# Three pieces of VectorE work in a two-layer attention kernel, moved to GpSimd and ScalarE

## The chip, the cores and the metric

The kernel runs on one core of one Trainium2 chip. A core has five engines with their own instruction queues, each in order: TensorE (PE in the profile; the loads of its weights, which run beside its matmuls, are listed as PEld), VectorE (DVE), ScalarE (ACT), GpSimd (POOL) and SyncE (SP), which here issues all transfers between HBM and the on-chip memory. The metric is device time of the whole program in microseconds. Before the change the median of three runs is 3306.71 us (3304.67 to 3315.07).

## What is computed

A step of a two-layer backbone on two streams: 256 prompt tokens and 2048 sample tokens, width 1024. The part of the reference that matters here:

```python
def _rmsnorm(x, g):
    xf = x.astype(jnp.float32)
    y = xf * lax.rsqrt(jnp.mean(xf * xf, axis=-1, keepdims=True) + EPS)
    return (y * g.astype(jnp.float32)).astype(x.dtype)
...
def _layer(x, mod, norm_g, w_in, ...):
    shift, scl, gate = jnp.split(mod, 3, axis=-1)
    xn = _rmsnorm(x, norm_g) * (1 + scl) + shift
    proj = xn @ w_in
    q, k, v, z_a, h_c, b_c, c_c, z_c, u_p, z_p = jnp.split(proj, SPLIT_IDX, axis=-1)
    ...
    attn = _attend(q, k_all, v_all) * jax.nn.silu(z_a)
    ...
    out = jnp.concatenate([attn, conv, pool], axis=-1) @ w_out
    return x + gate * out, k, v

def reference(x_prompt, x_sample, cache_k, cache_v, ...):
    ...
    for l in range(DEPTH):
        ...
        z, _, _ = _layer(z, mod, ...)
    y_sample = _rmsnorm(z, final_g)
```

There are 8 query heads of 64 columns that share 2 key and value heads. A sample token attends to 2304 keys (2048 of its own, 256 cached), a prompt token to the 256 of the prompt. Both streams end in a norm with final_g, here called the final norm.

## The kernel before

The program has four phases: for each layer a first one (norm, input projection, the conv and pool branches) and a second one (attention, output projection, and in the last layer the final norm). The first phase of the last layer begins while the tail of the first layer's attention runs.

The second phase works on 4 blocks of 512 query rows, each with 8 heads. One head of one block is a unit of 9 steps, a step being 256 keys; four units of one step carry the prompt's heads. That makes 292 steps per layer. One step has on TensorE four matmuls of scores (st, L1150 and L1151), four of the maxima that a coming unit needs (mx, L1111), and those with the values of the step three before (pv, L1196). ScalarE takes the exponential twice (L1160 and L1162), to P in float32 and ph in float16; ph has buffers for three steps. GpSimd subtracts, pl = P - ph, the low part of P (through the helper padd, L180, so that all its work carries that line), and adds up the pieces of the denominator Z that VectorE reduces (L1182). VectorE also takes the maxima (mr, L1112, from PSUM). At the end of a unit the products with pl follow (L1203).

After a pair of heads its output o is finished in four parts, one step apart, by fin_c: c1 multiplies by the reciprocal denominators on VectorE (L1254), c2 by the gate silu(z) on GpSimd (o<-o,zs), c3 casts the high part mixh on ScalarE (L1261), and c4 subtracts it from o on VectorE, which gives the low part mixl (L1266). There are 20 such pairs in a layer, 40 in the program. The output projection of a block (outproj) takes high and low parts as operands. It stands in a list from which one entry is taken per step: its matmuls read weights that SP loads on the way (wo); after each fourth entry VectorE adds the product to the residual (ox, L1327), and at the end of a quarter of the columns SP stores it.

In the last layer the final norm comes after a block's projection. ScalarE has squared the rows (L1330). The list called slow then gives one entry per step: first mean (L1349 to L1351: the sum over the squares, times 1/D, and the making of the list of the root's parts), then the 12 parts of the root's reciprocal (newton_parts, L144: the sum with EPS, a shift and a multiply-add on the bits, and three Newton steps of three instructions), all on VectorE with 4 columns of 128 rows, 2 columns in the prompt's block. Then for each 128 rows come two loads of 512 columns (oy), two empty entries, four scalings fin of 256 columns on VectorE (L1364: row factor times column factor fg) with a store after the second and the fourth, and empty entries. This happens in the loop for the prompt's block and the first two sample blocks; the root of the third falls into the tail, and the last block has its own tail (outproj_tail).

Of the kernel before, what the change touches and what calls it, by code (L numbers as in the profile page):

```python
# [19 lines left out]
D = 1024  # L20
# [75 lines left out]
def hybrid_step(ctx: ExitStack, tc: tile.TileContext, A, O):  # L96
# [82 lines left out]
    def padd(out, a, b, op=ALU.add):  # L179
        nc.gpsimd.tensor_tensor(out=out, in0=a, in1=b, op=op)  # L180
# [817 lines left out]
    def phase_b(l, xs_src, xp_src, xs_dst, xp_dst, nxt):  # L998
# [3 lines left out]
        with ExitStack() as st, ExitStack() as left:  # L1002
# [242 lines left out]
            def fin_c(zs, o, bc, B, pair):  # L1245
# [17 lines left out]
                def c4():  # L1263
                    h = st["h"]
                    lo = wk.tile([128, 512], F32R, tag="mixl", name="mixl", bufs=7)
                    nc.vector.tensor_tensor(out=lo[:, 0:n], in0=o[:, 0:n], in1=h[:, 0:n], op=ALU.subtract)  # L1266
                    B.mix[pair] = (h, lo)
# [7 lines left out]
            def outproj(B):  # L1275
# [68 lines left out]
                if last:  # L1344
                    out = (O["y_prompt"] if B.prompt else O["y_sample"])[0]

                    def mean():
                        s = sm.tile([128, 4], F32, tag="os", name="os")
                        nc.vector.tensor_reduce(out=s[:, 0:nt], in_=state["ss"][:, 0:nt, :], axis=AX.X, op=ALU.add)  # L1349
                        nc.vector.tensor_scalar(out=s[:, 0:nt], in0=s[:, 0:nt], scalar1=1.0 / D, scalar2=None, op0=ALU.mult)  # L1350
                        state["r"], state["newton"] = newton_parts(sm, s[:, 0:nt], nt, "or", EPS)  # L1351
# [7 lines left out]
                    def fin(t, i):  # L1359
                        r0 = B.t0 + t * 128  # L1360
                        y = state["y", t, i // 2]
                        c = slice(256 * i, 256 * i + 256)
                        yv = y[:, 256 * (i % 2):256 * (i % 2) + 256]
                        nc.vector.scalar_tensor_tensor(out=yv, in0=yv, scalar=state["r"][:, t:t + 1],  # L1364
                                                       in1=fg[:, c], op0=ALU.mult, op1=ALU.mult)
                        if i % 2:
                            nc.sync.dma_start(out=out[r0:r0 + 128, 256 * i - 256:256 * i + 256], in_=y)

                    light = [mean] + [lambda i=i: state["newton"][i]() for i in range(12)]
                    for t in range(nt):  # L1370
                        light.extend([lambda t=t, i=i: fin_load(t, i) for i in range(2)] + [lambda: None] * 2)
                        light.extend([lambda t=t, i=i: fin(t, i) for i in range(4)] + [lambda: None] * PR['lsp'])
# [331 lines left out]
```

## Time and profile before

| | before |
|---|---|
| median of three runs | 3306.71 us (3304.67 to 3315.07) |
| profiled execution, its own time | 3312.87 us |
| its span on the core | 3311.0 us |
| mean granted clock of TensorE | 0.976 |
| TensorE, weight loads | 94%, 74% |
| VectorE | 74% |
| GpSimd | 60% |
| ScalarE | 55% |

The shares are averages over the whole span. In a row of groups stand line, engine, operation, the tile written and those read, partitions x elements of output and input, the count, then busy time and the mean of one instruction, then the idle time of that engine just before these instructions and what ended most of it. A row of stretches has begin and end, length, the busy time of each engine with its instructions, and the mean granted clock of TensorE (1.00 is the full 2.4 GHz, 0.50 is 1.2 GHz). Work that is listed under a helper's line is told apart by its tiles.

### The profile page before, as it was taken

How to read it: one execution, taken by the hardware profiler on the slowest of the kernel's cores; microseconds unless marked ns; L12 is line 12 of the kernel's file. 1: busy time of each engine (PE TensorE's matmuls, PEld its weight loads, DVE VectorE, ACT ScalarE, POOL GpSimd, SP SyncE). 2: the span in 40 equal slices, each digit the busy share in tenths (PEclk: the TensorE clock that was granted, in tenths of full speed). 3: DMA queues.
4: the chain of work that ended last, by engine and by line, in shares of the span. 5: the costliest groups of instructions: out<-in, count | busy, mean ns of one | idle time of the engine just before them, and what ended most of it. 6: DMA issues, size and time to landing. Idle time of an engine off the chain costs nothing. (4 is left out here: it accounts for less than half of the span.)

```text
span 3311.0 us, 48199 instructions
## 1 busy us (share of the span) xinstructions
PE 3117.3 (94%) x17818; PEld 2457.1 (74%) x17818; DVE 2439.7 (74%) x3860; ACT 1821.6 (55%) x2610; POOL 1972.2 (60%) x1192
## 2 busy tenths in 40 slices
PE   7899999998999999999999999999899999999998
PEld 5788788765677777777789787987567676776777
DVE  5645565468888888888468546735888988999876
ACT  3223333247877777777533323323787776776773
POOL 2324363237887787887543435422787777777773
PEclk9899999999999999999999999999999999999999
DMA  7245744351342323243633554334223324233245
GB/s 242 73 139 181 244 134 135 115 154 32 93 143 59 102 77 99 55 126 98 201 118 96 182 189 147 121 105 109 57 80 122 106 78 119 74 116 92 75 145 201
DMA packets 367011, 400.02 MB, mean 121 GB/s; under 512 B 31028, under 2 KB 317240, under 8 KB 366008
## 3 DMA queue, kind: packets, MB, share of 16 engines
q1 hardware_dynamic: 366776, 396.94, 39.1%
q8 instruction: 142, 2.33, 0.3%
q14 instruction: 93, 0.76, 0.1%
HBM read 281.50 MB, written 115.36 MB: 120 GB/s over the span
## 5 line engine op out<-in xcount | busy, mean ns | idle before, releaser
L180 POOL TENSOR_TENSOR pl<-P,ph 128x1024 f16<-128x1024 f32 (+2 forms) x594 | 1247.5, 2113 | 325.3 <-ACT ph L1162 301.4
L1112 DVE TENSOR_REDUCE mr<-mx 128x1 f32<-128x512 f32 x1024 | 693.6, 683 | 213.0 <-PE mx L1111 207.1
L1160 ACT ACTIVATE P<-st 128x1024 f32<-128x1024 f32 x576 | 635.7, 1104 | 320.3 <-PE st L1151 313.3
L1182 DVE TENSOR_REDUCE Z<-P 128x152 f32<-128x912 f32 (+2 forms) x576 | 695.2, 1207 | 6.9 <-ACT P L1160 5.9
L1162 ACT ACTIVATE ph<-st 128x1024 f16<-128x1024 f32 x584 | 591.8, 1013 | 0.0
L1111 PE MATMUL mx<-KH,T 128*128 128x512 f32 x1024 | 494.1, 483 | 46.7 <-DVE mr L1112 33.7
L632 PE MATMUL rest<-xh,wh 128*128 128x512 f32 (+1 forms) x1280 | 485.6, 379 | 0.4 <-ACT xh L443 0.4
L634 PE MATMUL rest<-xh,wl 128*128 128x512 f32 (+1 forms) x1280 | 475.9, 372 | 5.1 <-DVE wl L427 3.2
L633 PE MATMUL rest<-xl,wh 128*128 128x512 f32 (+1 forms) x1280 | 476.2, 372 | 0.9 <-POOL xl L180 0.9
L1150 PE MATMUL st<-T,KH 128*128 128x512 f32 x1152 | 466.8, 405 | 3.1 <-ACT ph L1162 3.1
L1151 PE MATMUL st<-T,KL 65*128 65x512 f32 x1152 | 464.2, 403 | 0.0
L1196 PE MATMUL pv<-ph,V 128*128 128x512 f16 x1152 | 357.8, 393 | 8.8 <-DVE o L1215 6.1
L1111 PEld LDWEIGHTS mx<-KH,T 128*128 128x128 f32 x1024 | 197.1, 192 | 216.8 <-DVE mr L1112 112.9
L634 PEld LDWEIGHTS rest<-xh,wl 128*128 128x128 f32 x1280 | 243.5, 190 | 48.4 <-DVE wl L427 3.8
L632 PEld LDWEIGHTS rest<-xh,wh 128*128 128x128 f32 x1280 | 244.3, 191 | 45.7 <-issue 6.7
L633 PEld LDWEIGHTS rest<-xl,wh 128*128 128x128 f32 x1280 | 244.0, 191 | 38.4 <-POOL xl L180 1.2
L427 POOL TENSOR_TENSOR wl<-wf,wh 128x512 fp32r<-128x512 f32 x88 | 124.3, 1413 | 243.1 <-ACT wh L425 226.5
L1151 PEld LDWEIGHTS st<-T,KL 65*128 65x128 f32 x1152 | 221.8, 193 | 48.8
L1150 PEld LDWEIGHTS st<-T,KH 128*128 128x128 f32 x1152 | 222.6, 193 | 42.9 <-ACT ph L1162 6.1
L475 PE MATMUL qkv<-wl,xh 128*128 128x256 f32 x864 | 247.0, 286 | 4.4 <-DVE wl L427 3.2
L474 PE MATMUL qkv<-wh,xh 128*128 128x256 f32 x864 | 250.6, 290 | 0.0
L180 POOL TENSOR_TENSOR Z<-Z 128x512 f32<-128x512 f32 x128 | 166.5, 1300 | 136.6 <-DVE Z L1182 110.9
(228 smaller groups left out, 5740.1 us busy)
## 6 DMA issues: line engine op xcount, KB each, us to landing
wo<-woH SPq DMA_DIRECT2D x68, 512.0 KB
wo<-woL SPq DMA_DIRECT2D x68, 512.0 KB
wf<-in_w_in SPq DMA_DIRECT2D x50, 512.0 KB
wa<-in_w_ada SPq DMA_DIRECT2D x24, 1024.0 KB
wf<-in_w_in SPq DMA_DIRECT2D x19, 1024.0 KB
woH<-wgh SPq DMA_DIRECT2D x64, 256.0 KB
woL<-wgl SPq DMA_DIRECT2D x64, 256.0 KB
T<-qH SPq DMA_DIRECT2D x128, 128.0 KB
```

The lines of the kernel that those rows point to most:

```text
L180: nc.gpsimd.tensor_tensor(out=out, in0=a, in1=b, op=op)
L632: nc.tensor.matmul(out=ps[:, 0:b.n], lhsT=wh[:, k, ms], rhs=b.h[:, k, :], start=(k == 0), stop=False)
L633: nc.tensor.matmul(out=ps[:, 0:b.n], lhsT=wh[:, k, ms], rhs=b.l[:, k, :], start=False, stop=False)
L634: nc.tensor.matmul(out=ps[:, 0:b.n], lhsT=wl[:, k, ms], rhs=b.h[:, k, :], start=False, stop=(k == KD - 1))
L1111: nc.tensor.matmul(out=ps, lhsT=u.T1[:, q * 128:(q + 1) * 128], rhs=u.KH[u.g][:, c * 512:(c + 1) * 512])
L1112: nc.vector.reduce_max(out=mr[:, q, c:c + 1], in_=ps, axis=AX.X)
L1150: nc.tensor.matmul(out=ps[:, i, :], lhsT=u.KH[u.g][:, kt], rhs=u.T1, start=True, stop=False)
L1151: nc.tensor.matmul(out=ps[:, i, :], lhsT=u.KL[u.g][0:65, kt], rhs=u.T2, start=False, stop=True)
L1160: nc.scalar.activation(out=P, in_=ps, func=AF.Exp, scale=0.125)
L1162: nc.scalar.activation(out=ph, in_=ps, func=AF.Exp, scale=0.125)
L1182: nc.vector.tensor_reduce(out=z[:, c], in_=u.P[grp][:, 0:ns, c, :].rearrange("p s n t -> p n s t"), axis=AX.XY, op=ALU.add)
L1196: nc.tensor.matmul(out=u.po, lhsT=u.V[u.g][:, 2 * j + i, :], rhs=ph[:, i, :], start=(j == 0 and i == 0), stop=False)
```

## The change

Three pieces leave VectorE. The low part of the mix (c4) becomes a GpSimd subtraction, in both layers and for all 40 pairs of heads. The root's reciprocal in the loop keeps three VectorE instructions, the sum, the shift and the multiply-add; the scaling by 1/D with the addition of EPS, and the Newton steps (now of four instructions, three products and one multiply-add), go to GpSimd. Its list has 17 entries in place of 13. The scaling becomes one ScalarE multiplication by the row factor and one GpSimd product with fg, each 512 columns wide and each an entry, with the store behind the GpSimd product; there are four entries for 128 rows as before. The last block's own tail keeps its code, but its low parts come from the same c4.

```diff
@@ -1263,7 +1263,7 @@
                 def c4():
                     h = st["h"]
                     lo = wk.tile([128, 512], F32R, tag="mixl", name="mixl", bufs=7)
-                    nc.vector.tensor_tensor(out=lo[:, 0:n], in0=o[:, 0:n], in1=h[:, 0:n], op=ALU.subtract)
+                    padd(lo[:, 0:n], o[:, 0:n], h[:, 0:n], ALU.subtract)
                     B.mix[pair] = (h, lo)
 
                 return [c1, c2, c3, c4]
@@ -1344,11 +1344,24 @@
                 if last:
                     out = (O["y_prompt"] if B.prompt else O["y_sample"])[0]
 
-                    def mean():
-                        s = sm.tile([128, 4], F32, tag="os", name="os")
-                        nc.vector.tensor_reduce(out=s[:, 0:nt], in_=state["ss"][:, 0:nt, :], axis=AX.X, op=ALU.add)
-                        nc.vector.tensor_scalar(out=s[:, 0:nt], in0=s[:, 0:nt], scalar1=1.0 / D, scalar2=None, op0=ALU.mult)
-                        state["r"], state["newton"] = newton_parts(sm, s[:, 0:nt], nt, "or", EPS)
+                    def root_parts():
+
+                        s = sm.tile([128, 4], F32, tag="os", name="os")[:, 0:nt]
+                        v = sm.tile([128, 4], F32, tag="nt_v", name="nt_v")[:, 0:nt]
+                        t = sm.tile([128, 4], F32, tag="nt_t", name="nt_t")[:, 0:nt]
+                        y = state["r"] = sm.tile([128, 4], F32, tag="or", name="or")[:, 0:nt]
+                        ps = nc.gpsimd.tensor_scalar
+                        step = [lambda: padd(t, y, y, ALU.mult), lambda: padd(t, t, v, ALU.mult),
+                                lambda: ps(out=t, in0=t, scalar1=-0.5, scalar2=1.5, op0=ALU.mult, op1=ALU.add),
+                                lambda: padd(y, y, t, ALU.mult)]
+                        return [lambda: nc.vector.tensor_reduce(out=s, in_=state["ss"][:, 0:nt, :], axis=AX.X, op=ALU.add),
+                                lambda: ps(out=v, in0=s, scalar1=1.0 / D, scalar2=EPS, op0=ALU.mult, op1=ALU.add),
+                                lambda: nc.vector.tensor_scalar(
+                                    out=t.bitcast(I32), in0=v.bitcast(I32), scalar1=1, scalar2=None,
+                                    op0=ALU.logical_shift_right),
+                                lambda: nc.vector.tensor_scalar(
+                                    out=y.bitcast(I32), in0=t.bitcast(I32), scalar1=-1.0, scalar2=float(0x5F3759DF),
+                                    op0=ALU.mult, op1=ALU.add)] + step * 3
 
                     def fin_load(t, i):
                         r0 = B.t0 + t * 128
@@ -1356,20 +1369,21 @@
                         state["y", t, i] = y
                         nc.sync.dma_start(out=y, in_=dst[r0:r0 + 128, 512 * i:512 * i + 512])
 
-                    def fin(t, i):
+                    def fin(t, i, part):
                         r0 = B.t0 + t * 128
-                        y = state["y", t, i // 2]
-                        c = slice(256 * i, 256 * i + 256)
-                        yv = y[:, 256 * (i % 2):256 * (i % 2) + 256]
-                        nc.vector.scalar_tensor_tensor(out=yv, in0=yv, scalar=state["r"][:, t:t + 1],
-                                                       in1=fg[:, c], op0=ALU.mult, op1=ALU.mult)
-                        if i % 2:
-                            nc.sync.dma_start(out=out[r0:r0 + 128, 256 * i - 256:256 * i + 256], in_=y)
-
-                    light = [mean] + [lambda i=i: state["newton"][i]() for i in range(12)]
+                        y = state["y", t, i]
+                        c = slice(512 * i, 512 * i + 512)
+                        if part == 0:
+                            nc.scalar.mul(out=y, in_=y, mul=state["r"][:, t:t + 1])
+                            return
+                        padd(y, y, fg[:, c], ALU.mult)
+                        nc.sync.dma_start(out=out[r0:r0 + 128, c], in_=y)
+
+                    light = [lambda: state.update(root=root_parts())] + [lambda i=i: state["root"][i]() for i in range(16)]
                     for t in range(nt):
                         light.extend([lambda t=t, i=i: fin_load(t, i) for i in range(2)] + [lambda: None] * 2)
-                        light.extend([lambda t=t, i=i: fin(t, i) for i in range(4)] + [lambda: None] * PR['lsp'])
+                        light.extend([lambda t=t, i=i, p=p: fin(t, i, p) for i in range(2) for p in range(2)]
+                                     + [lambda: None] * PR['lsp'])
                     end = fns[-1]
                     fns[-1] = lambda: (end(), slow.add(light))
                 return start, fns
```

The order of VectorE's instructions in the first layer, around two low parts of a block (Z the pieces of the denominator, mr the maxima); lines with - stand only before, with + only after:

```order
 L1182 TENSOR_REDUCE Z<-P 128x170
-L1112 TENSOR_REDUCE mr<-mx 128x1
-L1266 TENSOR_TENSOR mixl<-o,mixh 128x256
-L1112 TENSOR_REDUCE mr<-mx 128x1
-L1182 TENSOR_REDUCE Z<-P 128x152
-L1112 TENSOR_REDUCE mr<-mx 128x1
-L1266 TENSOR_TENSOR mixl<-o,mixh 128x512
-L1112 TENSOR_REDUCE mr<-mx 128x1
+L1112 TENSOR_REDUCE mr<-mx 128x1 x2
+L1182 TENSOR_REDUCE Z<-P 128x152
+L1112 TENSOR_REDUCE mr<-mx 128x1 x2
 L1182 TENSOR_REDUCE Z<-P 128x190
```

The two subtractions between the maxima are gone from this queue, and nothing takes their place.

VectorE in the last layer, where the root of the first sample block begins, before (os is the sum, nt_v and nt_t are the root's small tiles, m and o belong to the attention beside it):

```order
L1349 TENSOR_REDUCE os<-oss 128x4
L1350 TENSOR_SCALAR os<-os 128x4
L1112 TENSOR_REDUCE mr<-mx 128x1
L1182 TENSOR_REDUCE Z<-P 128x170
L1112 TENSOR_REDUCE mr<-mx 128x1
L153 TENSOR_SCALAR nt_v<-os 128x4
L1128 TENSOR_REDUCE m<-mr 128x4
L1112 TENSOR_REDUCE mr<-mx 128x1
L1182 TENSOR_REDUCE Z<-P 128x152
L1112 TENSOR_REDUCE mr<-mx 128x1
L1254 TENSOR_TENSOR o<-o,rlb 128x512
L154 TENSOR_SCALAR nt_t<-nt_v 128x4
```

The same engine and place after the change (line numbers of the changed kernel; or is the root):

```order
L1357 TENSOR_REDUCE os<-oss 128x4
L1128 TENSOR_REDUCE m<-mr 128x4
L1112 TENSOR_REDUCE mr<-mx 128x1
L1182 TENSOR_REDUCE Z<-P 128x152
L1112 TENSOR_REDUCE mr<-mx 128x1
L1254 TENSOR_TENSOR o<-o,rlb 128x512
L1112 TENSOR_REDUCE mr<-mx 128x1
L1182 TENSOR_REDUCE Z<-P 128x190
L1112 TENSOR_REDUCE mr<-mx 128x1
L1359 TENSOR_SCALAR nt_t<-nt_v 128x4
L1112 TENSOR_REDUCE mr<-mx 128x1
```

Between the sum and the shift (L1359) no small instruction is left here; the nt_v that the shift reads is now made on GpSimd, and maxima stand behind the shift. GpSimd at this place after the change (pl is the low part of P):

```order
L180 TENSOR_TENSOR pl<-P,ph 128x1024 x6
L180 TENSOR_TENSOR o<-o,zs 128x512
L1358 TENSOR_SCALAR nt_v<-os 128x4
L180 TENSOR_TENSOR Z<-Z 128x512
L180 TENSOR_TENSOR pl<-P,ph 128x1024 x2
L180 TENSOR_TENSOR mixl<-o,mixh 128x512
L180 TENSOR_TENSOR pl<-P,ph 128x1024
L180 TENSOR_TENSOR nt_t<-or 128x4
```

The first instruction of the root stands behind a run of pl and the product with the gate, and the low part of the pair of heads stands between two pl.

GpSimd some steps later, where the scaling begins (oy holds 128 rows of the output, fg the column factors):

```order
L180 TENSOR_TENSOR pl<-P,ph 128x1024 x4
L180 TENSOR_TENSOR o<-o,zs 128x512
L180 TENSOR_TENSOR Z<-Z 128x512
L180 TENSOR_TENSOR pl<-P,ph 128x1024 x2
L180 TENSOR_TENSOR mixl<-o,mixh 128x512
L180 TENSOR_TENSOR oy<-oy,fg 128x512
L180 TENSOR_TENSOR pl<-P,ph 128x1024
L180 TENSOR_TENSOR Z<-Z 128x512
L180 TENSOR_TENSOR pl<-P,ph 128x1024
L180 TENSOR_TENSOR oy<-oy,fg 128x512
```

Each product with fg waits for its ScalarE multiplication, and the pl of the attention stand behind it.

## Rows read from the trace of the kernel before

**Rows 1.** The page: busy time of each engine, share of the span, instructions.

```profile
PE 3117.3 (94%) x17818; PEld 2457.1 (74%) x17818; DVE 2439.7 (74%) x3860; ACT 1821.6 (55%) x2610; POOL 1972.2 (60%) x1192
```

**Rows 2.** Stretches: blocks 1 to 3 of both layers; last columns DMA share, GB/s.

```profile
core 0: us, PE busy (x) PEld busy (x) DVE busy (x) ACT busy (x) POOL busy (x), PEclk, DMA share, GB/s
950.10:1591.10 641.00, 625.77 (x3570) 470.75 (x3568) 556.51 (x755) 479.69 (x586) 517.54 (x264) 1.00 0.32 94
2530.10:3221.10 691.00, 655.19 (x3570) 484.22 (x3568) 616.28 (x837) 500.01 (x683) 520.70 (x264) 0.96 0.34 103
```

**Rows 3.** Stretches: pairs of heads with a root, and theirs in the first layer.

```profile
950.10:1003.80 53.70, 51.88 (x283) 37.07 (x282) 48.05 (x67) 41.77 (x52) 44.54 (x24) 1.00 0.49 145
...
1396.90:1449.40 52.50, 50.60 (x272) 35.67 (x272) 47.08 (x66) 41.66 (x52) 45.19 (x25) 1.00 0.40 121
2530.10:2591.80 61.70, 56.94 (x283) 40.08 (x282) 55.97 (x78) 43.38 (x58) 45.00 (x24) 0.92 0.46 135
...
3006.50:3070.10 63.60, 57.26 (x271) 39.55 (x270) 57.99 (x79) 42.85 (x58) 45.36 (x24) 0.89 0.35 108
```

**Rows 4.** Single lines: duration ns min/median/max, first and last start us, forms.

```profile
L156 DVE TENSOR_SCALAR nt_y<-nt_t x3: 158/303/2098, 2566.6 to 3034.1; 128x4 int32<-128x4 int32 x2, 128x2 int32<-128x2 int32 x1
...
L1266 DVE TENSOR_TENSOR mixl<-o,mixh x40: 678/1698/2660, 770.5 to 3265.3; 128x512 fp32r<-128x512 f32 x32, 128x256 fp32r<-128x256 f32 x8
...
L1112 DVE TENSOR_REDUCE mr<-mx x1024: 669/681/693, 682.8 to 3207.0; 128x1 f32<-128x512 f32 x171
...
L154 DVE TENSOR_SCALAR nt_t<-nt_v x3: 155/158/1203, 2562.4 to 3030.9; 128x4 int32<-128x4 int32 x2, 128x2 int32<-128x2 int32 x1
...
L1470 ACT ACTIVATE ox<-ox,nt_y x4: 722/725/727, 3276.4 to 3306.7; 128x512 f32<-128x512 f32 x4
```

**Rows 5.** Timeline, first layer: start us, length us, engine, line; in brackets waits.

```profile
1258.55 6.86 POOL L180 TENSOR_TENSOR pl<-P,ph 128x1024 f16<-128x1024 f32 x3
...
1258.80 2.48 DVE L1266 TENSOR_TENSOR mixl<-o,mixh 128x512 fp32r<-128x512 f32 x1
...
1273.82 0.39 PE L1324 MATMUL op<-wo,mixh 128*128 128x256 f32 x1 [2.23 <-DMA wo<-woL]
```

**Rows 6.** Groups of VectorE by form, 2530.1 to 3221.1 us (last layer).

```profile
L1364 DVE SCALAR_TENSOR_TENSOR oy<-oy,nt_y,fg 128x256 f32<-128x256 f32 x40 | 38.8, 970 | 0.0
...
L1254 DVE TENSOR_TENSOR o<-o,rlb 128x512 f32<-128x512 f32 x12 | 8.1, 677 | 1.7 <-PE rlb L1253 1.7
```

**Rows 7.** Groups of GpSimd by form, the same stretch.

```profile
L180 POOL TENSOR_TENSOR pl<-P,ph 128x1024 f16<-128x1024 f32 x207 | 451.5, 2192 | 104.6 <-ACT ph L1162 95.3 <-PE mx L1111 3.4 <-PE st L1151 2.3
...
L180 POOL TENSOR_TENSOR o<-o,zs 128x512 f32<-128x512 f32 x11 | 14.2, 1286 | 0.0
```

**Rows 8.** Stretches, VectorE alone: tile os, tile nt_t, then line L1266.

```profile
2530.10:3221.10 691.00, 6.26 (x9) 0.96 0.34 103
...
2530.10:3221.10 691.00, 28.93 (x33) 0.96 0.34 103
...
950.10:1591.10 641.00, 24.73 (x11) 1.00 0.32 94
```

**Rows 9.** Groups of the whole program, shapes together.

```profile
L1266 DVE TENSOR_TENSOR mixl<-o,mixh 128x512 fp32r<-128x512 f32 (+1 forms) x40 | 68.7, 1717 | 3.0 <-ACT mixh L1261 3.0
L180 POOL TENSOR_TENSOR o<-o,zs 128x512 f32<-128x512 f32 (+1 forms) x40 | 47.4, 1185 | 19.5 <-DVE o L1254 11.2 <-DVE nt_t L151 8.3
L1203 PE MATMUL pv<-pl,V 128*64 128x512 f16 x1152 | 142.7, 393 | 0.1
```

**Rows 10.** Groups of ScalarE, 2530.1 to 3221.1 us.

```profile
L1160 ACT ACTIVATE P<-st 128x1024 f32<-128x1024 f32 x206 | 227.0, 1102 | 127.6 <-PE st L1151 125.6
L1162 ACT ACTIVATE ph<-st 128x1024 f16<-128x1024 f32 x207 | 209.4, 1012 | 0.0
```

**Rows 11.** Waits of TensorE, 950.1 to 1591.1: us in total, times, longest.

```profile
PE op L1324 <- DMA wo<-woL: 5.8, 5, 2.2
PE mx L1111 <- DVE mr L1112: 3.9, 8, 0.8
```

**Rows 12.** Waits of SP's queue, whole program: us in total, times, longest.

```profile
SPq L1367 <- DVE oy L1364: 199.7, 22, 42.6
```

## The prediction

> **What bounds the kernel now.** I read the views in this order: busy shares of the page, a table of stretches, the costliest groups of VectorE, a timeline of two places, and the waits of TensorE. The page says TensorE 94%, VectorE 74%, GpSimd 60%, ScalarE 55% [rows 1], which alone would put VectorE off the path. The stretches say otherwise. The attention loop runs twice, once in each layer, with the same matmuls: 3570 in the stretch of blocks 1 to 3 of either layer [rows 2]. It takes 641.0 us in the first layer and 691.0 us in the last; VectorE is busy 556.5 and 616.3 us. TensorE is busy 625.8 of 641.0 us in the first layer, so little is left to win there. The last layer is 50.0 us longer, and what it has more is the final norm, with a few squares and transfers. The reader can so price the final norm by subtraction, one layer from the other.
>
> Where the 50.0 us lie: there are three pairs of heads in which the roots are worked out; the first and the last of them take 61.7 and 63.6 us, against 53.7 and 52.5 us in the first layer [rows 3], the three together 28.9 us more, with a granted clock of 0.92 and 0.89 against 1.00. The other 21.1 us fall to the rest of the stretch, where the scaling of the outputs stands.
>
> Why small instructions cost so much shows in their times. A VectorE instruction on 4 columns (nt_y, L156) takes between 158 and 2098 ns; the low part of the mix (mixl, L1266) 678 to 2660 ns [rows 4]. The long ones stand beside a GpSimd subtraction (pl): in the timeline mixl begins at 1258.80, in the middle of a run of pl that began at 1258.55, and takes 2.48 us [rows 5]. The multiplication by the reciprocals (L1254), of the same width but with one operand in PSUM, takes 677 ns in the last layer [rows 6], and the maxima (L1112, one operand) 669 to 693 ns all through the program [rows 4]. So VectorE's instructions with two operands in SBUF, and small ones with a scalar, are held up by GpSimd; the rest aren't. The page "SBUF — State Buffer" of the Trainium skill (section "Who interferes with whom") says the same and adds that a GpSimd instruction which has begun keeps the port to its end; the trace agrees, as the longest small instruction (2098 ns) is near the mean of pl, 2192 ns [rows 4, 7].
>
> How a hold-up reaches TensorE: the queue of VectorE is in order, so behind mixl waits the addition of the output projection (ox), behind that SP's store of it, and behind that the load of the next weights (wo), for which TensorE sits 2.23 us at 1273.82 [rows 5].
>
> **The change part by part.** *Roots.* In the loop there are three (the prompt's, blocks 0's and 1's); a fourth is in the tail. Each is 14 VectorE instructions; 42 took 6.26 + 28.93 = 35.2 us [rows 8]. After, each leaves a reduction (one operand; taken at 0.16 us, the shortest small one [rows 4]), a shift and a multiply-add on VectorE. The last two stay exposed: now they take 1.5 and 2.6 us in three roots, the sums of L154 and L156 [rows 4]; bounds for the six are 6 x 0.16 = 1 and 6 x 2.1 = 12.6 us; I take the 4.1 measured. New is that the shift waits for GpSimd's v, which stands behind a pl in its queue: nothing to one pl (2.2 us) each, I take 3 us for three; behind the shift wait the maxima, and TensorE for them. So 0.5 + 4.1 + 3 = 7.6 of 35.2 us stay and the excess of 28.9 us falls by 78%: **22.7 us** (12 to 28). GpSimd gets 13 instructions of 2 or 4 columns a root. It takes 1.29 us for 512 columns [rows 7]; the 40 of its multiplications by the gate, 32 of 512 and 8 of 256, take 47.4 us [rows 9], so one of 256 takes (47.4 - 32 x 1.286) / 8 = 0.78 us, and by the slope one of few columns some 0.3 us, an estimate from these two rows; with no small TENSOR_SCALAR on GpSimd in the trace I allow 0.1 to 1 us. They stand one in a step, in GpSimd's idle time.
>
> *Scaling.* 40 instructions in the loop (16 more in the tail) took 38.8 us, mean 970 ns [rows 6]. They go; 20 ScalarE multiplications of 0.725 us (14.5 us; the tail has such ones, L1470 [rows 4]) and 20 GpSimd ones of 1.29 us (26 us) come. ScalarE sits 125.6 us of the 691 idle for scores from TensorE [rows 10], so 14.5 us are hidden there; without that cover they would delay the exponentials by as much. Of the 21.1 us I take back **15** (8 to 21): the squares and the transfers of the final norm stay.
>
> *Low part of the mix.* 40 instructions, 68.7 us of VectorE, mean 1.717 us, in both layers; on GpSimd they are 47.4 us, as many and as wide as the multiplications by the gate [rows 9]. What a microsecond of it is worth I take from the first layer, which has no other moved part: 11 of them took 24.73 us [rows 8], while matmuls waited 5.8 us for wo and 3.9 for maxima [rows 11], 9.7 us or 0.39 of it. Upper bound: all of TensorE's 15.2 us of idle time there [rows 2], 0.61; lower: the maxima alone, 0.16. With the 0.39: **27 us** (11 to 42) over the program.
>
> *What GpSimd's longer queue costs.* In the stretch of the last layer it is busy 520.7 of 691.0 us [rows 2] and gets 14 + 26 + 8 = 48 us. Its pl are needed late: TensorE hardly waited for one, 0.1 us idle before all 1152 products of the low part [rows 9], and ScalarE never waited for a buffer of ph (idle 0.0) [rows 10]. The stores of the outputs now wait on SP for GpSimd's product in place of VectorE's; SP already stood 199.7 us for the latter [rows 12], and loads of wo are queued behind. I take **5 us** lost (0 to 20).
>
> One rule speaks against the move. The page "Perfetto Trace Analysis" of the Trainium skill (section "Optimizing Scalar/DVE Operations") says that GpSimd and VectorE share a read port of SBUF, so that moving work between them may not help. It would give the second rival below; by the control rows of L1254 and L1112 it binds few of the instructions that are left.
>
> *The tail* after 3221 us: its last low part costs 1.29 us in place of 0.68 at most, and the final chain of one-column steps stays as it is. I take 0.
>
> **Sum.** 22.7 + 15 + 27 - 5 = 60 us. The profiled execution took 3312.87 us with a span of 3311.0, so 3253 for such a one; the median of the three runs is 6.2 us lower, 3306.71 - 60 = **3247 us**. Ends: 12 + 11 + 8 - 20 = 11, so 3296; 28 + 42 + 21 = 91, so 3216.
>
> **Rivals.**
> 1. *All of it comes back* (gain near 90, 3217 us): VectorE's hold-ups were the only stalls, and the shift never waits. For: the clock fell only where VectorE was late [rows 3]. Against: the weights' loads and TensorE at 97% in the first layer.
> 2. *The port is shared whoever works* (gain 28, 3279 us): GpSimd works 81 us more in all (47 + 26 + 8) and holds up VectorE's reductions by as much; at 0.39 this gives 32 us of the 60 back. Against: L1112's 669 to 693 ns beside pl [rows 4].
> 3. *GpSimd becomes the bound; slower* (3323 us). If GpSimd's idle time before Z and pl is only waiting for late inputs, it has no slack; then its 81 us lie on the path against the 22.7 + 15 + 27 = 65 us above, +16. It decides from the point where GpSimd is over two steps behind, so that ScalarE waits for a ph buffer of three. For: the stretch leaves it at 569 us of some 640, 89%. Against: no such wait shows now [rows 9, 10]. The page "GPSIMD Engine Reference" of the Trainium skill (section "Engine selection") is on this side: elementwise work belongs on VectorE, GpSimd being about half as fast. The rows show 1.29 us on GpSimd against a mean of 1.717 us on VectorE, and 0.68 us only where nothing held it up [rows 4, 7, 9].
> 4. *It does nothing* (3307 us): TensorE's own queue sets the pace and other waits take the places.
>
> **Chances.** Forecast (gain 40 to 80) 0.60, rival 1 0.12, rival 2 0.16, rival 3 0.06, rival 4 0.06. The forecast alone spans 3227 to 3267; with the ends of the unknown costs and rival 2 the range is 3214 to 3290. A measurement of this kernel can tell about 0.3%, 10 us, from no change; so faster 0.88, same 0.06, slower 0.06.
>
> **What would show it.** The stretch of the last layer should shrink to some 645 us, that of the first to some 631; the three root pairs to 54 to 57 us with a granted clock near 1.00; VectorE's group of L1266 and L1364 gone, no small VectorE instruction but shift and multiply-add above 1 us. Wrong I would be if ScalarE shows idle time before ph, if TensorE waits for pl, if a POOL TENSOR_SCALAR of 4 columns takes microseconds, or if the maxima grow beyond 0.69 us.

## The result and the profile after

The changed kernel takes 3279.47 us (median of four runs, 3275.13 to 3281.21) against 3306.53 us before (four runs): ratio 0.9911, 95% interval 0.9891 to 0.9931. That is 27 us less. The forecast was 60 us less, 3247 us: the sign was right, the size off by more than a factor of two. The profiled execution has a span of 3278.7 us, 32.3 us under that of before, and all comparisons of stretches below are between profiled executions. The profiled one of before took 6 us more than the median of its kernel, that of the changed kernel 1 us more, so 5 of the 32.3 us are the choice of executions.

The page after, busy time of each engine as in [rows 1]:

```profile
PE 3098.1 (94%) x17818; PEld 2453.5 (75%) x17818; DVE 2311.2 (70%) x3720; ACT 1836.7 (56%) x2638; POOL 2046.3 (62%) x1312
```

VectorE has 128 us less work, GpSimd 74 us more. The stretches after, first the two of [rows 2] (blocks 1 to 3 of the first and of the last layer, up to the first scores of the layer's last unit), then the three root pairs of the last layer, of which two stand in [rows 3]:

```profile
944.00:1580.10 636.10, 624.20 (x3568) 470.97 (x3567) 533.78 (x744) 479.48 (x586) 527.30 (x275) 1.00 0.32 95
2519.00:3177.70 658.70, 636.62 (x3570) 477.41 (x3568) 537.25 (x753) 510.42 (x703) 557.56 (x334) 0.98 0.35 108
...
2519.00:2576.10 57.10, 55.16 (x284) 39.28 (x283) 46.98 (x69) 43.39 (x58) 46.79 (x31) 0.94 0.49 146
2744.20:2798.40 54.20, 51.42 (x277) 36.33 (x277) 47.46 (x67) 42.47 (x58) 46.82 (x31) 1.00 0.43 127
2975.10:3028.80 53.70, 51.02 (x271) 35.40 (x270) 47.38 (x67) 42.54 (x58) 47.05 (x32) 1.00 0.43 128
```

The first layer's stretch is 4.9 us shorter, the last layer's 32.3 us; of these 24.1 us are the three root pairs, 165.0 us where they were 189.1. The granted clock is back at 1.00 in two of the pairs and at 0.94 in the first. Against this stands the end of the program: from the last unit's first scores to the end it took 89.9 us (3221.1 to 3311.0) and takes 101.0 us (3177.7 to 3278.7), 11.1 us more. The sum of these three is 26.1 us less; the other 6 us of the 32.3 were saved before and between these stretches, 3.6 of them before the attention begins, where the change touches nothing.

The waits of TensorE after, first layer (944.0 to 1580.1), to be read beside [rows 11]:

```profile
PE op L1324 <- DMA wo<-woL: 4.8, 5, 1.6
PE mx L1111 <- DVE mr L1112: 3.3, 5, 1.1
```

All low parts are off VectorE, and in this pair of executions the waits for wo and for the maxima are nearly what they were. The last layer, first before (2530.1 to 3221.1):

```profile
PE mx L1111 <- DVE mr L1112: 15.4, 25, 2.2
...
PE op L1324 <- DMA wo<-woL: 4.9, 4, 1.7
...
PE op L1323 <- DMA wo<-woH: 0.5, 1, 0.5
```

And after the change (2519.0 to 3177.7):

```profile
PE op L1324 <- DMA wo<-woL: 7.2, 7, 2.2
PE mx L1111 <- DVE mr L1112: 5.4, 10, 1.2
PE op L1323 <- DMA wo<-woH: 5.2, 2, 2.6
```

The waits for maxima are a third of the 15.4 us they had been there, but those for wo have grown from 5.4 to 12.4 us. A place where it happens is at 3101 us: GpSimd's product with fg, SP's queue, and the matmul that waits (timelines of three engines; columns as in [rows 5], and SPq marks a transfer that SP issues):

```profile
3100.37 1.28 POOL L180 TENSOR_TENSOR oy<-oy,fg 128x512 f32<-128x512 f32 x1
...
3094.21 0.60 SPq L177 DMA_DIRECT2D T<-qL  x1
3101.68 0.34 SPq L1380 DMA_DIRECT2D out_y_sample<-oy  x1
3102.12 0.38 SPq L177 DMA_DIRECT2D wo<-woH  x1
3102.60 0.51 SPq L177 DMA_DIRECT2D wo<-woL  x1
...
3107.38 0.35 PE L1323 MATMUL op<-wo,ch 128*128 128x256 f32 x1 [2.54 <-DMA wo<-woH]
3108.75 0.58 PE L1324 MATMUL op<-wo,ch 128*128 128x256 f32 x1 [1.01 <-DMA wo<-woL]
```

SP stands from 3094.81 on, 6.9 us; the store starts when the product ends (3101.65), and the weights behind it go out only then. They need no product at all. The second of them lands some 6 us after its issue (3102.60 to 3108.75).

### The profile page after: what moved, and what is told of

Read it like the earlier page. It is cut to its first block, busy times and chain, and to the rows that moved or that the text cites. A ratio compares the mean times of both kernels' runs of the same rounds, so it can differ in the third digit from the quotient of the medians.

```text
span 3278.7 us, 48192 instructions
## 1 busy us (share of the span) xinstructions
PE 3098.1 (94%) x17818; PEld 2453.5 (75%) x17818; DVE 2311.2 (70%) x3720; ACT 1836.7 (56%) x2638; POOL 2046.3 (62%) x1312
## 5 line engine op out<-in xcount | busy, mean ns | idle before, releaser
L1160 ACT ACTIVATE P<-st 128x1024 f32<-128x1024 f32 x576 | 636.1, 1104 | 300.4 <-PE st L1151 295.6
L1182 DVE TENSOR_REDUCE Z<-P 128x152 f32<-128x912 f32 (+2 forms) x576 | 696.2, 1209 | 6.6 <-ACT P L1160 5.5
L476 PE MATMUL qkv<-wh,xl 128*128 128x256 f32 x864 | 245.4, 284 | 0.0
```

What stands on the lines that cost most here:

```text
L1160: nc.scalar.activation(out=P, in_=ps, func=AF.Exp, scale=0.125)
L1182: nc.vector.tensor_reduce(out=z[:, c], in_=u.P[grp][:, 0:ns, c, :].rearrange("p s n t -> p n s t"), axis=AX.XY, op=ALU.add)
```

## The experiments

Each kernel was timed against the kernel before on the same chip; medians and ratios are those of its own comparison. The median of the kernel before differs between these comparisons (3306.53, 3311.33, 3313.1 and 3313.85 us), so kernels of different comparisons are set side by side by their gain over their own before, which is 27 us for the changed kernel. The first theory was that the low part had been priced too high and that the scaling on ScalarE holds up the tail; the rival was the second of the prediction, that GpSimd's added work gives back what VectorE gains.

**The three parts, each alone on the kernel before.** The low part:

```diff
-                    nc.vector.tensor_tensor(out=lo[:, 0:n], in0=o[:, 0:n], in1=h[:, 0:n], op=ALU.subtract)
+                    padd(lo[:, 0:n], o[:, 0:n], h[:, 0:n], ALU.subtract)
```

> The kernel before with only the low part of the mix on GpSimd. The forecast's term was 27 us for both layers, so about 3280 us. New theory: the trace after shows the first layer's blocks 1 to 3 only 4.9 us shorter with 11 low parts moved, because the waits for weights and maxima in that stretch were not caused by the low parts; by that some 0.45 us for each of 40, a gain of 10 to 18 us in all, 3289 to 3297 us, with TensorE's waits for wo still above 4 us in the first layer. Rival (GpSimd's longer queue costs as much as VectorE gains): no gain, 3302 to 3310 us, with ScalarE or TensorE waiting for GpSimd.

Measured: 3291.87 against 3311.33 us, ratio 0.9944 (0.9924 to 0.9963), 19 us less. No wait of TensorE for GpSimd is listed in the last layer's stretch. The rival falls; the price lies between the new theory's and the forecast's.

The new theory rested on one pair of executions, and the stretch differs between executions. Nine of the kernels here differ in the first layer in the low part alone. There the stretch took 641.0, 645.4, 649.2 and 645.6 us in the four with the low part on VectorE (before, and root_alone, fin_alone and root_alone_13 below), and 636.1, 636.6, 639.3, 634.7 and 638.3 us in the five without it (after, mix_alone, and tail_scaling_on_vector, after_13 and late_store below). The means are 8.3 us apart where the one pair gave 4.9, and the waits for wo are 7.3 us on average in the four and 4.0 in the five: somewhat under half of these waits went with the low part, the rest did not. One wait of 1.4 us for ox, which stood behind the low part in VectorE's queue, goes in all five.

The roots alone (root_parts of the diff with before's fin):

> The kernel before with only the root's reciprocals moved to GpSimd (shift and multiply-add stay on VectorE), scaling and low part as before. Forecast's term and new theory agree: 20 to 26 us gain, 3281 to 3287 us, the three pairs of heads with a root at 55 to 58 us in place of 61.7 to 63.8. Rival (small GpSimd instructions and the shift's wait cost what VectorE saves): under 10 us.

Measured: 3323.86 against 3311.33 us, ratio 1.0038 (1.0024 to 1.0053): 13 us slower, where forecast and new theory had a gain of 20 to 26 us and the rival one of under 10. Yet the root pairs are 22.5 us shorter, as forecast. The loss is elsewhere: the stretches between and after the root pairs, where the scaling stands, take 184.7, 190.1 and 157.8 us in place of 175.8, 175.1 and 151.0, and the end 98.6 us in place of 89.9. The scaling on VectorE in blocks 1 to 3, before at 970 ns each [rows 6], and a wait of TensorE there (lc are the matmuls of the denominators; they write to the PSUM buffers of the maxima and so wait until VectorE has read these):

```profile
L1377 DVE SCALAR_TENSOR_TENSOR oy<-oy,or,fg 128x256 f32<-128x256 f32 x40 | 51.1, 1278 | 0.3 <-issue 0.3
...
PE lc L1230 <- DVE mr L1120: 17.7, 12, 2.5
```

And three units of block 2 in a row (stretches; columns as in [rows 2]):

```profile
2884.50:2918.90 34.40, 31.29 (x164) 23.61 (x163) 29.96 (x38) 21.29 (x30) 22.49 (x12) 0.90 0.21 68
2918.90:2952.50 33.60, 29.71 (x156) 21.64 (x155) 31.02 (x39) 22.08 (x33) 23.63 (x13) 0.95 0.40 120
2952.50:2986.80 34.30, 31.68 (x164) 23.86 (x164) 27.77 (x37) 21.52 (x30) 22.32 (x12) 0.90 0.34 109
```

The same units took 28.6, 29.8 and 29.1 us before, at clock 1.00. The same 40 instructions became a third dearer, and with the waits the granted clock fell to 0.90 to 0.95.

The scaling alone (the new fin behind before's roots):

> The kernel before with only the scaling moved (ScalarE times root, GpSimd times column factor, 512 wide); roots and low part on VectorE. Forecast's term: 15 us, 3292 us. New theory: 5 to 12 us won in the loop, and about 9 us lost in the tail, where the scaling of the third block waits for its loads at the head of ScalarE's queue and the squares of the last block stand behind it: 3300 to 3311 us, with the time from the last cast of mixh to the end some 9 us above the 46.4 us of before. If the tail's loss comes from the longer list of the root instead, that time stays near 46 us here.

Measured: 3316.63 against 3311.33 us, ratio 1.0009 (0.9994 to 1.0025): no change, and above the band of the new theory. But the end took 91.1 us, and the time from the last cast (of mixh) to the end 47.8 us, not 55: my explanation of the tail fails here. The loop has waits for wo instead, 16.9 us in blocks 1 to 3 of the last layer where there were 5.4:

```profile
PE op L1324 <- DMA wo<-woL: 9.8, 8, 2.9
PE op L1323 <- DMA wo<-woH: 7.1, 2, 4.8
```

**The tail's scaling back on VectorE**, all else as changed (an instruction of 512 columns in place of the multiplication and the product):

```diff
-                        if part == 0:
+                        if not B.prompt and B.t0 == 1024:
+                            if part == 0:
+                                nc.vector.scalar_tensor_tensor(out=y, in0=y, scalar=state["r"][:, t:t + 1],
+                                                               in1=fg[:, c], op0=ALU.mult, op1=ALU.mult)
+                                return
+                        elif part == 0:
                             nc.scalar.mul(out=y, in_=y, mul=state["r"][:, t:t + 1])
                             return
-                        padd(y, y, fg[:, c], ALU.mult)
+                        else:
+                            padd(y, y, fg[:, c], ALU.mult)
```

> The changed kernel, but the third sample block's scaling (the one that falls into the tail) is one 512-wide VectorE instruction again; its store stands where it stood. New theory (ScalarE's queue holds the tail): the time from the last cast of mixh to the end falls from 55.3 us to 46 to 49 us, 3270 to 3274 us in all. Rival (the root's 17 entries on GpSimd or the later list make the tail long): within 3 us of the changed kernel, 3276 to 3282 us.

Measured: 3274.1 against 3311.33 us, ratio 0.9895 (0.9877 to 0.9913). Cast to end 51.4 us, the end 97.1 us, neither in the theory's 46 to 49 us nor where the rival had it: ScalarE's queue holds 4 of the 11 us at most. With the two runs before, the tail's loss follows the root's list, which is 17 entries long in root_alone (98.6 us) and 13 in fin_alone (91.1 us). This holds in all kernels of this document: the end took 97.1 to 101.0 us in the five with 17 entries and 89.7 to 92.1 us in the nine with 13.

**The list cut to 13 entries.** In root_alone and in the changed kernel (cuts within the diff are marked ...):

```diff
-                        step = [lambda: padd(t, y, y, ALU.mult), lambda: padd(t, t, v, ALU.mult),
+                        def square():
+                            padd(t, y, y, ALU.mult)
+                            padd(t, t, v, ALU.mult)
+
+                        step = [square,
...
-                        return [lambda: nc.vector.tensor_reduce(out=s, in_=state["ss"][:, 0:nt, :], axis=AX.X, op=ALU.add),
-                                lambda: ps(out=v, in0=s, scalar1=1.0 / D, scalar2=EPS, op0=ALU.mult, op1=ALU.add),
+                        nc.vector.tensor_reduce(out=s, in_=state["ss"][:, 0:nt, :], axis=AX.X, op=ALU.add)
+                        return [lambda: ps(out=v, in0=s, scalar1=1.0 / D, scalar2=EPS, op0=ALU.mult, op1=ALU.add),
...
-                    light = [lambda: state.update(root=root_parts())] + [lambda i=i: state["root"][i]() for i in range(16)]
+                    light = [lambda: state.update(root=root_parts())] + [lambda i=i: state["root"][i]() for i in range(12)]
```

> root_alone with its list cut from 17 to 13 entries (the sum in the entry that makes the list, the two products of a Newton step in one entry), so that everything behind the root stands at the steps of before. root_alone won 22.5 us in its three root pairs and lost 30.7 us in the stretches of the scaling and 8.7 in the tail. Theory: the four entries did that, since the scalings met other pl and the tail's loads fell behind the residual's loads in SP's queue; then the stretches return to about 176, 175 and 151 us, the tail to 90, and the time is 3284 to 3294 us. Rival: GpSimd's small instructions themselves delay pl and with it TensorE; then it stays above 3312 us.

Measured: 3286.12 against 3313.1 us, ratio 0.9911 (0.9893 to 0.993). The same instructions on the same engines as in root_alone, four entries earlier: a loss of 13 us has become a gain of 27, some 39 us, and the roots alone are then worth as much as the whole change. The stretches are 174.0, 173.0 and 146.2 us, the end 90.6. The scaling there:

```profile
L1381 DVE SCALAR_TENSOR_TENSOR oy<-oy,or,fg 128x256 f32<-128x256 f32 x40 | 34.8, 871 | 0.0
...
PE lc L1230 <- DVE mr L1120: 1.3, 4, 0.8
```

> The changed kernel with its root's list cut to 13 entries in the same way. Theory: the tail (from the last unit's first scores to the end) falls from 101.0 to 90 to 93 us, the rest stays within 5 us: 3264 to 3274 us. Rival (the tail is long because ScalarE's multiplications and GpSimd's products wait for loads in it): 97 us and more, 3274 to 3282 us.

Measured: 3275.29 against 3313.1 us, ratio 0.9877 (0.9859 to 0.9895), 38 us less and so 11 more than the changed kernel gained. The end is 91.3 us, as the theory had it and not the rival, but the time misses the theory's band by 1 us: blocks 1 to 3 of the last layer are 6.7 us longer than after the change, where at most 5 were allowed, and waits for wo there are 17.5 us in place of 12.4. SP's queue in the tail shows what the four entries did; before, after, and with 13 entries (oy the loads of rows to be scaled, ox those of the residual for the last block):

```profile
3255.75 3.89 SPq L1357 DMA_DIRECT2D oy<-xS  x2
3259.69 6.64 SPq L1388 DMA_DIRECT2D ox<-xS  x4
```

```profile
3214.68 11.02 SPq L1402 DMA_DIRECT2D ox<-xS  x4
3226.04 0.79 SPq L1370 DMA_DIRECT2D oy<-xS  x2
```

```profile
3221.33 3.90 SPq L1374 DMA_DIRECT2D oy<-xS  x2
3225.27 5.87 SPq L1406 DMA_DIRECT2D ox<-xS  x4
```

With 17 entries the first rows of the third block are asked for behind the residual, 2.7 us after the last cast (3223.4) where it had been 8.9 us ahead of it (3264.6), and the first of the scaled rows is stored 15.7 us after that cast (3239.09) in place of 8.7 (3273.32), beside the last block's own chain.

**The two stores later.** In the changed kernel the stores move into the two empty entries behind the scaling:

```diff
-                        padd(y, y, fg[:, c], ALU.mult)
+                        if part == 1:
+                            padd(y, y, fg[:, c], ALU.mult)
+                            return
                         nc.sync.dma_start(out=out[r0:r0 + 128, c], in_=y)
...
-                                     + [lambda: None] * PR['lsp'])
+                                     + [lambda t=t, i=i: fin(t, i, 2) for i in range(2)])
```

> The changed kernel with the two stores of the scaled rows 3 and 2 entries later (in the two empty entries), so that SP reaches them when GpSimd's product is done. Theory: TensorE's waits for wo in the last layer's loop (12.4 us in blocks 1 to 3) come from SP standing at these stores; they fall to 3 to 7 us, the loop becomes 5 to 15 us shorter, 3264 to 3274 us. Rival (wo waits come from the store of ox or from the wo buffers): no change within 4 us.

Measured: 3262.77 against 3313.1 us, ratio 0.9845 (0.9828 to 0.9861), below the expected band. The gain is 50 us. The last layer's blocks 1 to 3 take 641.3 us, 17.4 less than after the change, with

```profile
PE mx L1111 <- DVE mr L1112: 5.4, 10, 1.2
PE op L1324 <- DMA wo<-woL: 3.1, 5, 1.0
```

So with 9.3 us less of waits for wo the stretch is 17.4 us shorter. The one unit of above, after the change, and then with the late stores, shows where the rest comes from:

```profile
3086.60:3122.00 35.40, 31.78 (x170) 24.34 (x169) 24.22 (x35) 22.94 (x32) 24.24 (x14) 0.90 0.45 138
```

```profile
3080.50:3109.80 29.30, 28.50 (x170) 22.28 (x169) 23.97 (x34) 22.78 (x32) 24.98 (x14) 1.00 0.48 160
```

The unit is 6.1 us longer with the stores where they were. Of these, 2.8 us are idle time of TensorE (3.6 us, the waits of 2.54 and 1.01, against 0.8); the other 3.3 us are busy time, the same 170 matmuls at a granted clock of 0.90 on the mean of the unit. After the two waits it stood at 0.50, the lower of the two levels (1.2 GHz), from 3110 to 3114 us, and at 1.00 again from 3116 on. Not every wait does this: the single one of 2.23 us in [rows 5] left it at 1.00 throughout (1266 to 1286 us).

**The weights ahead of the store of ox**, in the changed kernel, both layers:

```diff
                         if t == nt - 1:
+                            if c + 1 < 4:
+                                load_c(c + 1, 0)
                             nc.sync.dma_start(out=dst[rows, c * 256:(c + 1) * 256].rearrange("(t p) n -> p t n", p=128),
...
-                                if t == nt - 1 and q % 2 == 1 and c + 1 < 4:
+                                if t == nt - 1 and q == 1 and c + 1 < 4:
```

> The changed kernel with the load of the next weights issued ahead of the store of ox instead of behind it, in both layers. Theory: in the first layer the 4.8 us of waits for wo come from SP standing at that store, which waits for VectorE's ox, not from the low parts; they fall below 1 us and the first layer's blocks 1 to 3 get 4 to 8 us shorter; the last layer too by some us: 3262 to 3274 us. Rival (the weights wait for their buffers or for the transfer's own time): no change within 4 us.

Measured: 3265.93 against 3313.1 us, ratio 0.9857 (0.9838 to 0.9875), a gain of 47 us. In the first layer no wait for wo is left, and the first waits of the list are

```profile
PE mx L1111 <- DVE mr L1112: 3.3, 5, 1.1
PE lc L1230 <- DVE mr L1120: 0.9, 5, 0.2
```

The stretch takes 630.8 us, 5.3 less, and the two kernels below that have this order too and no low part on VectorE take 630.8 and 630.7. These waits had been there with the low parts gone; their cause is the store of ox in SP's queue. The last layer's stretch is 9.5 us shorter, 649.2 us, with 7.2 us of waits for wo left.

**All three edits on the changed kernel.**

> The changed kernel with the three edits that each took away one loss: the root's list of 13 entries, the late stores, the weights ahead of the store of ox. If the losses are separate, the first layer's blocks 1 to 3 take about 631 us (as weights_before_ox_store), those of the last layer 634 to 641 (late_store 641.3), the end 90 to 92 (after_13), and the time is 3235 to 3250 us. If the stalls only move on (each edit won by chance of place), it stays above 3258 us.

Measured: 3246.24 against 3313.85 us, ratio 0.9797 (0.9773 to 0.9822), a gain of 68 us, the largest here. The end is 91.3 us, and all the expected bands are met. The two stretches of [rows 2] in it:

```profile
947.80:1578.60 630.80, 623.46 (x3568) 470.92 (x3567) 533.37 (x744) 479.40 (x586) 526.68 (x275) 1.00 0.32 96
2514.70:3153.10 638.40, 628.57 (x3568) 472.20 (x3567) 537.17 (x753) 510.61 (x703) 557.34 (x334) 0.99 0.36 111
```

The last layer costs only 7.6 us more than the first; it had been 50.0 us.

**SP's two edits on the kernel before, with nothing moved.** The edits are the last two diffs, the store as a function of its own because before's scaling has four parts.

> The kernel before, nothing moved between engines, with only the two edits on SP's queue (late stores, weights ahead of the store of ox). Theory: SP's stalls and VectorE's hold-ups are separate losses; TensorE's waits for wo (5.8 and 5.4 us in the two layers) go, the waits for maxima stay: 3288 to 3304 us, and the change is worth 45 to 60 us on top (three_edits against this one). Rival (the move of the work is worth little and SP was all of it): under 3275 us.

Measured: 3295.38 against 3313.85 us, ratio 0.9946 (0.9925 to 0.9967). In the last layer (2519.6 to 3198.9) the waits for wo fall to 0.7 us and those for VectorE stay:

```profile
PE mx L1111 <- DVE mr L1112: 18.2, 33, 2.2
PE lc L1230 <- DVE mr L1120: 7.8, 7, 2.2
PE rlb L1253 <- DVE mr L1112: 3.7, 2, 2.3
...
PE op L1324 <- DMA wo<-woL: 0.7, 1, 0.7
```

So the move with a list of 13 entries and SP's queue out of the way is worth 3295.38 - 3246.24 = 49 us, and the rival falls. Neither loss is the other, but they are not independent: the move with 13 entries alone gains 38 us (after_13) and SP's two edits alone 18, 56 together, where both at once gain 68. The moved products had made SP stand longer, as the waits for wo of 17.5 us in after_13 show.

**Single parts priced on three_edits.** The low part back on VectorE:

> three_edits with the low part of the mix back on VectorE. The forecast's term for it was 27 us, mix_alone gave about 19 with SP's stalls in place. If wo waits were part of what the low part cost, it costs less now: 8 to 20 us over three_edits. If the forecast's price holds, 27 or more.

Measured: 3264.45 against 3313.85 us, ratio 0.9841 (0.9817 to 0.9865), 18 us over three_edits. In the stretches of blocks 1 to 3 only 3.3 us (first layer) and 4.7 (last) of it are seen; the rest lies in block 0 of both layers and in between, where single executions of kernels that do the same there differ by up to 9 us. What sets those was not settled. The two stretches hold 22 of the 40 low parts, so by their share their 8.0 us make some 15 us of the program (an estimate), and the price is 15 to 18 us.

The scaling back on VectorE:

> three_edits with the scaling back on VectorE (four instructions of 256 columns for 128 rows; order of SP's queue unchanged). The forecast's term was 15 us. fin_alone moved it and won nothing, with wo waits of 17 us; with SP's stalls gone I expect 5 to 15 us over three_edits. Rival (ScalarE and GpSimd lose as much as VectorE gains): within 4 us of three_edits.

Measured: 3247.87 against 3313.85 us, ratio 0.9799 (0.9778 to 0.9821), 1.6 us over three_edits. In the last layer's stretch it is 7.5 us (645.9 against 638.4). The rival's bound of 4 us holds in the medians, which can't tell 7 us apart well; the forecast's 15 is excluded by both.

## Why the prediction was off, step by step

- *Roots, 22.7 us*: right, and for the stated reason. 24.1 us measured in the three pairs, 22.5 with the roots alone. The bounds of the working held too: VectorE sat 4.2 us before the three shifts (I had taken 3, at most 6.6), the shift took 170 ns each and the multiply-adds 0.5 to 1.2 us. The last layer, line L1359 with what it waited for, and L1362:

```profile
L1359 DVE TENSOR_SCALAR nt_t<-nt_v x3: 170/170/170, 2553.6 to 3000.4; 128x4 int32<-128x4 int32 x2, 128x2 int32<-128x2 int32 x1
...
  POOL nt_v L1358: 4.2, 3
...
L1362 DVE TENSOR_SCALAR or<-nt_t x3: 534/1093/1181, 2556.7 to 3002.8; 128x4 int32<-128x4 int32 x2, 128x2 int32<-128x2 int32 x1
```

- *The tail, 0*: the step that failed outright. "The final chain of one-column steps stays as it is" looked at instructions and not at the list they stand in: four more entries put the third block's loads behind others in SP's queue. It cost 11.1 us, of which the list of 13 entries gives back 9.7. The front of the document had the 17 and 13 entries; the sum had no term for them, in the tail or in the loop. In root_alone the four entries cost some 39 us.
- *GpSimd's longer queue, 5 us*: the mechanism was named (stores wait on SP, loads of wo behind them), the size was wrong. Waits for wo grew by 7.0 us, and the late stores, which also take out part of the old ones, return 17.4 us: the unit at 3101 us shows that such waits can cost clock as well as idle time.
- *Low part, 27 us*: too high by some 8 to 12 us, though well inside its own 11 to 42. It measured 19 us alone (12 to 25 by the interval) and 15 to 18 with SP's queue out of the way. 0.39 us per us rested on all waits for wo and maxima of the first layer being the low part's; on average over the executions above 4.0 of 7.3 us for wo stayed when it was gone, and they went with SP's order alone. The stretch gave 8.3 us on average for 11 low parts of 24 us, 0.35 per us, and with SP's new order 3.3, 0.13 per us.
- *Scaling, 15 us*: mis-sized; nothing when moved alone with its stores where they were (fin_alone), 2 us by the medians and 7.5 in the stretch with SP's queue out of the way. I had put the remainder of 21.1 us (last layer less first, outside the root pairs) down to the scaling. It is 14 us with SP's two edits alone, 9 in three_edits_scaling_back and 2 in three_edits: a third of it was SP's order and about a third the scaling. These are single executions, so a few us each are uncertain.
- *The sum.* By the medians, and with 13 entries, the low part alone gains 19 us and the roots 27, and the scaling loses 5, which makes 41 in all, and 38 together (after_13); the four entries then cost 11. Against the forecast's 60 the low part is 8 us short, scaling and stores together, 15 - 5 = 10, give nothing, and the tail takes 11: 29 of the 33 us that are missing.
- *What would show it.* The root pairs came to 53.7 to 57.1 us, forecast 54 to 57; the stretches to 636.1 and 658.7 us in place of 631 and 645.
- *Rivals.* The first (gain 90) and the fourth (none) are excluded by the measured gain of 23 to 36 us. The second named the measured time, 3279 us, with the wrong cause: VectorE's instructions with an operand in PSUM or only one operand were not slower with GpSimd at 557.56 of 658.70 us. The reductions of Z (L1182) took 1207 ns on average before and 1209 after. After the change the maxima and the multiplications by the reciprocals:

```profile
L1112 DVE TENSOR_REDUCE mr<-mx x1024: 669/683/694, 679.6 to 3163.6; 128x1 f32<-128x512 f32 x171
...
L1254 DVE TENSOR_TENSOR o<-o,rlb x40: 408/677/689, 760.4 to 3221.3; 128x512 f32<-128x512 f32 x32, 128x256 f32<-128x256 f32 x8
```

  That is [rows 4, 6] again. That rival's agreement with the time is chance. The third (GpSimd the bound) is off as well; ScalarE's ph never waited for a buffer in the last layer's stretch after the change:

```profile
L1162 ACT ACTIVATE ph<-st 128x1024 f16<-128x1024 f32 x207 | 209.7, 1013 | 0.0
```

With the three edits, which take out the tail's loss and the waits for wo in both layers, the kernel stands at 3246 us, one us from the forecast's 3247. That is no proof of it, and the nearness is chance: the kernel before took 3313.85 us in that comparison, so the gain is 68 us and not 60; the forecast's terms for low part and scaling were too high; and SP's two edits, which give 18 us on the kernel before, were no part of the change.

## What to carry to other kernels

Where work is handed out one list entry per step, count the entries that a change adds as carefully as the microseconds: they move everything behind them in the list, whichever engine runs it. A store issued in an in-order queue right behind the instruction that makes its data holds up every load behind it; issue it when the data is there, and loads that need nothing first. A wait seen in a stretch is not the wait of the instruction you want to move until it goes with that instruction. And one pair of executions is not enough to price a few us in a stretch of 640: stretches that run the same code differed here by up to 8 us.

## What the hardware showed that was not expected

The scaling of 256 columns on VectorE took 1278, 970, 891, 871, 863 or 847 ns on average in six kernels with the same 40 instructions (root_alone, before, before_sp_edits, root_alone_13, mix_alone, three_edits_scaling_back). What differs is where it stands among GpSimd's work; that this place sets its length fits the rows but was not tried by itself. GpSimd's instructions on 2 or 4 columns took 0.19 to 0.20 us there, below the estimate of 0.3, and its products of 512 columns kept the 1.29 us of [rows 7] (groups of the last layer's stretch after the change):

```profile
L180 POOL TENSOR_TENSOR oy<-oy,fg 128x512 f32<-128x512 f32 x20 | 25.9, 1296 | 0.0
...
L180 POOL TENSOR_TENSOR mixl<-o,mixh 128x512 fp32r<-128x512 f32 x11 | 14.1, 1281 | 0.0
L180 POOL TENSOR_TENSOR nt_t<-nt_t,nt_v 128x4 f32<-128x4 f32 x6 | 1.2, 204 | 0.0
...
L1355 POOL TENSOR_SCALAR nt_t<-nt_t 128x4 f32<-128x4 f32 x6 | 1.2, 194 | 0.0
```
